# Seven products of a pair in one run: moving the next pair's early products, and the layout of the seeded PSUM banks

## The chip, the cores and the metric

The kernel runs on one core of a Trainium2 chip. The metric is device time in microseconds of one execution. The engines are TensorE (PE; its weight loads are listed as PEld), VectorE (DVE), ScalarE (ACT), GpSimd (POOL) and SyncE (SP), which only starts DMAs here. [...]

## The reference

One step of a single-layer encoder: 512 prompt frames and 64 sample frames, model width 1024, hidden width 4096. After two kinds of attention comes the part that matters here, the feed-forward layer:

```python
x = layer_norm(ALPHA * x + jnp.einsum('blm,md->bld', mix, w_o), ln1_g, ln1_b)
hid = jnp.square(jax.nn.relu(jnp.einsum('bld,df->blf', x, w_up)))
x = layer_norm(ALPHA * x + jnp.einsum('blf,fd->bld', hid, w_down), ln2_g, ln2_b)
gate = jax.nn.sigmoid(jnp.einsum('bld,de->ble', x, w_ple_gate) + b_ple_gate)
```

All of it is f32. The kernel splits each operand into a high and a low part and makes each f32 product from three TensorE passes (high x high, high x low, low x high).

## The kernel before, in words

The 576 frames are two halves A and B of 288 columns. Most of the feed-forward layer is done with Winograd's form of Strassen's product: a block product of 2 x 2 blocks takes seven products instead of eight. A **pair** is one such block product for 256 output rows (two blocks of 128) and both halves. `up_pair` makes hidden rows from x, `down_pair` adds hidden rows times `w_down` into Y. The hidden width is cut into eight groups g of 512. The list `todo` has 24 pairs: four down pairs (hidden groups 0 and 1), then three times four up pairs (g = 2, 3; then 4, 5; then 6, 7; two pairs per group), the first two times followed by four down pairs. Groups 6 and 7 are multiplied by `w_down` in the ordinary way behind the phase (tiles hidE and hidO).

The seven products of a pair have names. Each is 12 matmuls of 128 x 288 into one PSUM bank (four blocks of k, three passes). P.o takes "11", and "t1" and "t2" are added to it (bank n in the profile, two buffers). P.z takes "t0". P.d starts as a copy of P.o after "11" (ACT, line 1466), and "21" is added to it. P.e starts as minus P.o after "t1" (ACT, line 1468); "t3" is added, then DVE reads it, then "22" is added and it is read again. z, d and e all lie in tiles that the profile calls g. Such a g tile has two banks; there are three of them, one from `psB` and two from the ring `psM`.

What reads the banks hangs on `P.posts` and is queued with `later` or `owe`: a queue of work that the loop takes up at its next steps. For an up pair ACT and DVE make relu, square, the sums for the next block product and their high and low parts (tiles hA to hD, hF, r; lines 1325 to 1355); for a down pair DVE adds into Y (lines 1549 to 1564).

Weights come as raw tiles by DMA (`wraw`). A **seven-product** weight has four units u to u+3: "11" and "21" use unit u, "t0" and "t3" u+1, "t1" and "t2" u+2, "22" u+3. For each unit ACT casts the high part (line 149) and DVE subtracts for the low part (line 155), into one of five `whl` slots; DVE also adds raw halves for u+2 (lines 181 and 184). `WT.step()` issues such pieces while products run. A unit may take a slot once the oldest unit still needed is fewer than five behind; `last_use` moves that on after "21", "t3", "t2" and "22".

The products stay in the order in which `seven` issues them (`pin`). Each engine does its own queue in order. Before the change the next pair's "11" and "t0" were taken ahead, between the products of this pair; the first down pair after up pairs (`turn`) has an order and a place for d of its own.

## Time and profile before

| | us |
|---|---|
| median of 3 runs | 784.63 (784.26 to 785.0) |
| the profiled execution | 783.34 |
| its span, first to last instruction | 781.6 |
| PE busy in the span | 755.0 (97%) |
| DVE, ACT busy | 581.2 (74%), 465.5 (60%) |
| seven-product phase, from and to | 382.23 to 672.79 |
| mean granted TensorE clock | 0.990 |

Rows of a timeline give start, duration, engine, line, operation, out<-in, and in brackets the idle time of that engine just before and what ended it. Rows of waits give the total, the number of times and the longest. Rows of windows give the length, each engine's busy time with its instructions in brackets, the granted clock, the DMA share and GB/s.

### The profile page before, as it was taken

What the parts mean: (1) busy time and instruction counts of PE and PEld (TensorE: products, weight loads), DVE (VectorE), ACT (ScalarE), POOL (GpSimd) and SP (SyncE); (2) the same over time, 40 slices, a digit from 0 to 9 for tenths busy, and PEclk for the clock granted to TensorE, in tenths of its full rate; (3) what the DMA queues carried; (4) which work ended last, traced back from release to release, by engine and by line L of the source; (5) the groups of instructions that cost most, each with busy time, mean ns of one, the idle gap of its engine ahead of it and who ended that gap; (6) DMA issues with size and microseconds to landing.
All of it is one profiled execution on the core that took longest, in us unless ns stands there. A gap on an engine that the chain in (4) does not pass through costs nothing.

```text
span 781.6 us, 14647 instructions
## 1 busy us (share of the span) xinstructions
PE 755.0 (97%) x5679; PEld 734.4 (94%) x5679; DVE 581.2 (74%) x1149; ACT 465.5 (60%) x921; POOL 110.1 (14%) x130
## 2 busy tenths in 40 slices
PE   9999999999999999999999996999969999999997
PEld 7999988998999999999899996999969999999997
DVE  6788888888668667988776689665895767658653
ACT  6579767887777433787634566336664366625451
POOL 7100324334321000100000000000000000010100
PEclk9999999999999999999999998999989999999999
DMA  8548354354213235355347664476654764741002
GB/s 279 176 61 171 98 144 129 101 173 129 94 58 117 62 91 167 117 139 130 73 123 185 163 161 123 122 184 160 161 131 122 169 165 139 263 151 32 28 28 68
DMA packets 38200, 101.37 MB, mean 130 GB/s; under 512 B 6001, under 2 KB 10225, under 8 KB 38001
## 3 DMA queue, kind: packets, MB, share of 16 engines
q1 hardware_dynamic: 34384, 87.61, 37.6%
q0 software_dynamic: 3456, 12.58, 9.1%
q8 instruction: 45, 0.74, 0.4%
q10 hardware_dynamic: 288, 0.22, 0.1%
q14 instruction: 27, 0.21, 0.1%
HBM read 85.26 MB, written 9.54 MB: 121 GB/s over the span
## 4 chain that ended last, share of the span: by engine, by line
PE 76%; DVE 15%; ACT 7%; issue 2%; DMA 1%; ACTq 0%; DVEq 0%
PE g L288 40%; PE n L288 14%; PE m L288 13%; DVE dbias L693 2%; PE T L56 2%; ACT xr L771 2%; DVE whl L155 1%; DVE m L691 1%; ACT whl L149 1%; PE V L958 1%; PE m L452 1%; DVE sP L891 1%; PE m L466 1%; DVE x L774 1%; PE S L883 1%
## 5 line engine op out<-in xcount | busy, mean ns | idle before, releaser
L149 ACT CAST whl<-wraw 128x1024 fp32r<-128x1024 f32 (+2 forms) x190 | 154.7, 827 | 112.5 <-PE g L288 81.4
L155 DVE TENSOR_TENSOR whl<-wraw,whl 128x1024 fp32r<-128x1024 f32 (+2 forms) x158 | 158.2, 1008 | 49.5 <-ACT whl L149 49.4
L288 PE MATMUL m<-AH,whl 128*128 128x288 f32 x736 | 176.6, 307 | 0.0
L288 PE MATMUL g<-BH,whl 128*128 128x288 f32 (+2 forms) x768 | 157.6, 296 | 0.0
L288 PEld LDWEIGHTS m<-AH,whl 128*128 128x128 f32 x736 | 126.4, 188 | 1.7 <-issue 1.0
L288 PEld LDWEIGHTS g<-BH,whl 128*128 128x128 f32 x768 | 124.4, 188 | 0.4 <-DVE whl L155 0.2
L288 PE MATMUL g<-BL,whl 128*128 128x288 f32 (+2 forms) x384 | 113.0, 295 | 0.0
L288 PE MATMUL m<-AL,whl 128*128 128x288 f32 x368 | 108.7, 295 | 0.0
L288 PEld LDWEIGHTS g<-BL,whl 128*128 128x128 f32 x384 | 72.3, 188 | 0.2
L288 PEld LDWEIGHTS m<-AL,whl 128*128 128x128 f32 x368 | 69.5, 189 | 0.7
L210 POOL DMA_DIRECT2D wraw<-in_w_dram x24 | 20.8, 866 | 302.9 <-DMA wraw<-in_w_dram 171.0
L896 ACT ACTIVATE sP<-sP,st 128x128 f32<-128x128 f32 (+4 forms) x72 | 39.4, 549 | 35.5 <-DVE st L891 35.4
L155 POOL TENSOR_TENSOR whl<-wraw,whl 128x512 fp32r<-128x512 f32 x32 | 42.3, 1335 | 90.1 <-ACT whl L149 85.3
L288 PE MATMUL m<-BH,whl 128*128 128x288 f32 x192 | 43.0, 302 | 0.0
L288 PE MATMUL g<-s,whl 128*128 128x288 f32 x288 | 42.2, 295 | 0.0
L288 PE MATMUL n<-BH,whl 128*128 128x288 f32 x192 | 42.1, 295 | 0.0
L288 PEld LDWEIGHTS g<-s,whl 128*128 128x128 f32 x288 | 39.5, 188 | 0.2 <-ACT g L1468 0.2
L288 PE MATMUL n<-hA,whl 128*128 128x288 f32 x144 | 24.8, 322 | 11.9 <-DVE whl L155 8.3
L288 PEld LDWEIGHTS n<-hA,whl 128*128 128x128 f32 x144 | 21.9, 207 | 13.8 <-DVE whl L155 9.3
L56 PE MATMUL T<-ident,sP 128*128 128x128 f32 (+1 forms) x176 | 31.3, 273 | 1.5 <-DVE sP L905 0.6
L288 PEld LDWEIGHTS m<-BH,whl 128*128 128x128 f32 x192 | 32.0, 188 | 0.5 <-issue 0.3
L288 PEld LDWEIGHTS n<-BH,whl 128*128 128x128 f32 x192 | 32.0, 188 | 0.0
(322 smaller groups left out, 1623.3 us busy)
## 6 DMA issues: line engine op xcount, KB each, us to landing
wraw<-in_w_dram SPq DMA_DIRECT2D x48, 512.0 KB, 3.7
wraw<-in_w_dram POOLq DMA_DIRECT2D x24, 512.0 KB, 7.2
wraw<-in_w_qkv_dram SPq DMA_DIRECT2D x23, 512.0 KB, 3.7
wraw<-in_w_dram SPq DMA_DIRECT2D x24, 256.0 KB, 6.5
wraw<-in_w_up_dram SPq DMA_DIRECT2D x8, 512.0 KB, 3.5
wraw<-in_w_down_dram SPq DMA_DIRECT2D x8, 512.0 KB, 3.4
wraw<-in_w_gate_dram SPq DMA_DIRECT2D x8, 512.0 KB, 4.8
wraw<-in_w_o_dram SPq DMA_DIRECT2D x8, 384.0 KB, 3.0
```

The costliest lines, as they stand in the source:

```text
L56: PE.transpose(out, in_, ident[:n, :n])
L149: ACT.copy(self.hv[u][:, 0, c], src["tile"][:, c])
L155: eng.tensor_tensor(t[:, 1, c], src["tile"][:, c], f(t[:, 0, c]), OP.subtract)
L210: POOL.dma_start(t[:, :n], it["acc"], accum_op=OP.add)
L288: mm = PE.matmul(ps, W(w, kw, wc), a[:, ka, cols], start=(first and i == 0), stop=(last and i == n - 1), skip_group_check=more)
L452: PE.matmul(mk[:, h, :HW], w0(part, k), a[:, k, h * HW:(h + 1) * HW], start=(k == 0 and i == 0), stop=(k == 7 and i == 2))
L466: PE.matmul(acc[b][:n[b], :304], a[:, k, b * 128:b * 128 + n[b]], ixw(part, k), start=(k == 0 and i == 0), stop=(k == 7 and i == 2))
L691: tc.keep_in_program_order(DVE.max(m, s))
L693: tc.keep_in_program_order(DVE.match_replace(out=s, in_to_replace=m, in_values=s, imm_value=GONE))
L771: q(lambda r=r, s=s: ACT.mul(v2(xr[r * 32:r * 32 + 32]), v[s * 32:s * 32 + 32], sc))
L774: q(lambda: DVE.tensor_tensor(x32, x32, xr, OP.add), 3)
L896: ACT.activation(j["P"], j["P"], AF.Exp, bias=j["st"][:, 0:1], scale=-1.0, accum_out=j["st"][:, 2:3])
```

## The change

Each pair's seven products now follow each other: "11", "t0", "t1", "21", "t3", "t2", "22". Nothing of the next pair comes between. The special order and place of `turn` are gone. z has a `psB` tile of its own use; e of a pair and d of the next pair are the two banks of one `psM` tile: `seeds[0]` is made at "t1", its bank 0 is this pair's e, and its bank 1 is the d that the next pair's "11" seeds. The reads of d and e, which were one instruction over both banks in most pairs, are two: d after "21", e after "22".

```diff
             if n == "11":
                 P.o = psum_n()[:, :HW]
-            if n == ("11" if P.turn else "t0"):
-                P.g = psB.tile([128, 2, 512], F32, name="g", tag="g", bufs=1)
-                P.z = P.g[:, 0, :HW]
+            elif n == "t0":
+                P.z = psB.tile([128, 2, 512], F32, name="g", tag="g", bufs=1)[:, 0, :HW]
...
             if n == "11":
-                P.m = psM.tile([128, 2, 512], F32, name="g", tag="m", bufs=2)
-                P.d, P.e = P.g[:, 1, :HW] if P.turn else P.m[:, 0, :HW], P.m[:, 1, :HW]
+                P.d = seeds[0][:, 1, :HW]
                 ACT.copy(P.d, P.o)
             elif n == "t1":
+                seeds[0] = psM.tile([128, 2, 512], F32, name="g", tag="m", bufs=2)
+                P.e = seeds[0][:, 0, :HW]
                 ACT.mul(P.e, P.o, -1.0)
...
-        yield from product(pairs[0], "11")
-        yield from product(pairs[0], "t0")
-        for i, P in enumerate(pairs):
+        seeds = [psM.tile([128, 2, 512], F32, name="g", tag="m", bufs=2)]
+        for P in pairs:
             if P.start:
                 P.start()
-            for n in ("11+", "t1", "21", "t3", "t2", "t0+", "22") if P.turn else ("21", "t1", "11+", "t3", "t2", "t0+", "22"):
-                if n[-1] != "+":
-                    yield from product(P, n)
-                elif i + 1 < len(pairs):
-                    yield from product(pairs[i + 1], n[:2])
+            for n in ("11", "t0", "t1", "21", "t3", "t2", "22"):
+                yield from product(P, n)
...
+        def s21():
+            later(0, lambda: ACT.activation(P.r[:, 0, 0], P.d, AF.Relu))
+
         def s22():
-            later(0, lambda: ACT.activation(P.r[:, 0], v2(P.m), AF.Relu))
+            later(0, lambda: ACT.activation(P.r[:, 0, 1], P.e, AF.Relu))
...
         def s21():
-            if P.turn:
-                later(0, lambda: begin(ya[:, 0], P.d, OP.add))
+            later(0, lambda: begin(y00, P.d, OP.add))
 
         def s22():
-            if P.turn:
-                later(0, lambda: begin(ya[:, 1], P.e, OP.add))
-            else:
-                later(0, lambda: begin(ya, v2(P.m), OP.add))
+            later(0, lambda: begin(y10, P.e, OP.add))
```

Three places in the built order. The first is TensorE's queue at the start of the phase, as a piece of the difference. A row is a product: n is bank o, g is z, d or e; hA to hD hold the hidden operands ("11" and "t0" read hA, "t1" and "t3" hC, "21" and "t2" hB, "22" hD).

```order
 L288 MATMUL n<-hA,whl 128x288 x12
 L288 MATMUL g<-hA,whl 128x288 x12
-L288 MATMUL n<-hA,whl 128x288 x12
 L288 MATMUL n<-hC,whl 128x288 x12
 L288 MATMUL g<-hB,whl 128x288 x12
 L288 MATMUL g<-hC,whl 128x288 x12
 L288 MATMUL n<-hB,whl 128x288 x12
+L288 MATMUL g<-hD,whl 128x288 x12
+L288 MATMUL n<-hA,whl 128x288 x12
 L288 MATMUL g<-hA,whl 128x288 x12
```

The second pair's "11" moved from the third place to behind the first pair's "22"; between the first pair's "11" and its "t1" only "t0" is left, and between "t3" and "22" only "t2".

The second place is ACT's queue at the first seam from up pairs to down pairs, from the last weight casts of the fourth up pair into the first down pair. Before:

```order
L149 CAST whl_5965<-wraw_5865 128x512
L149 CAST whl_5954<-wraw_5738 128x1024
L1327 CAST hB_5716<-r_5827 128x576
L1327 CAST hC_5814<-hF_5475 128x576
L149 CAST whl_5981<-wraw_5870 128x1024
L1327 CAST hC_5814<-hF_5475 128x576
L1536 ACTIVATE r_5827<-g_5776 128x576
L1537 ACTIVATE r_5827<-r_5827 128x576
L1327 CAST hB_5716<-r_5827 128x576
L1327 CAST hD_5815<-r_5827 128x576
L1466 COPY g_6009<-n_5979 128x288
```

Now:

```order
L149 CAST whl_5967<-wraw_5868 128x512
L1532 ACTIVATE r_5861<-g_5884 128x288
L149 CAST whl_6005<-wraw_5873 128x1024
L1533 ACTIVATE r_5861<-r_5861 128x576
L1327 CAST hB_5687<-r_5861 128x576
L1327 CAST hC_5804<-hF_5444 128x576 x2
L1327 CAST hB_5687<-r_5861 128x576
L1464 COPY g_5884<-n_5949 128x288
L1468 ACTIVATE g_6015<-n_5949 128x288
L1327 CAST hD_5805<-r_5861 128x576
```

whl_5981 before and whl_6005 now are the weights of the second down pair's "11". The copy now belongs to the first down pair itself, whose "t1" is two products behind its "11"; before, the copy in this place was the second down pair's.

The third place is DVE's queue in the first up pair behind the down pairs: the first r<-g row is the read of e after "t3", for which "22" waits. Before:

```order
L155 TENSOR_TENSOR whl_5520<-wraw_5375,whl_5520 128x1024
L184 TENSOR_TENSOR wraw_5378<-wraw_5378 128x512
L1524 TENSOR_TENSOR r_5457<-g_5412,r_5457 128x288
L155 TENSOR_TENSOR whl_5574<-wraw_5378,whl_5574 128x1024
L1527 TENSOR_TENSOR r_5457<-n_5395,r_5457 128x288
```

Now:

```order
L184 TENSOR_TENSOR wraw_5372<-wraw_5372 128x512
L155 TENSOR_TENSOR whl_5537<-wraw_5369,whl_5537 128x1024
L1517 TENSOR_TENSOR r_5479<-g_5502,r_5479 128x288
L155 TENSOR_TENSOR whl_5570<-wraw_5372,whl_5570 128x1024
L1520 TENSOR_TENSOR r_5479<-n_5445,r_5479 128x288
```

The read of e now stands directly behind a 1024-wide weight split, with the sums of raw halves ahead of both.

## The prediction

> **What bounds the kernel now.** I read the page's engine table first, then TensorE's waits from 340 to 700 us, then TensorE's timeline through the seven-product phase, and last ScalarE's (ACT) and VectorE's (DVE) timelines around the places where TensorE stands still. All of them are views of the kernel before.

> ```profile
> PE 755.0 (97%) x5679; PEld 734.4 (94%) x5679; DVE 581.2 (74%) x1149; ACT 465.5 (60%) x921; POOL 110.1 (14%) x130
> ...
> PE n L288 <- DVE whl L155: 8.3, 4, 3.4
> PE n L288 <- ACT whl L149: 3.6, 4, 1.1
> PE g L288 <- DVE Y L1553: 2.1, 1, 2.1
> PE g L288 <- ACT g L1466: 1.0, 1, 1.0
> ```

> TensorE bounds the program, so a change to the order of products can gain only what TensorE loses there. The ten waits sum to 15.0 us; 11.9 of it is product "11" (into a tile n) waiting for a weight split. The timeline shows what the waits cost in all:

> ```profile
> 382.23 1.75 PE L288 MATMUL n<-hA,whl 128*128 128x288 f32 x12
> 384.95 1.86 PE L288 MATMUL g<-hA,whl 128*128 128x288 f32 x12 [0.97 <-ACT g L1466]
> 392.08 1.87 PE L288 MATMUL g<-hB,whl 128*128 128x288 f32 x12 [2.08 <-DVE Y L1553]
> 393.79 1.76 PE L288 MATMUL g<-hC,whl 128*128 128x288 f32 x12
> 400.18 1.76 PE L288 MATMUL g<-hB,whl 128*128 128x288 f32 x12
> 422.52 1.76 PE L288 MATMUL g<-hB,whl 128*128 128x288 f32 x12
> 476.98 1.75 PE L288 MATMUL g<-hA,whl 128*128 128x288 f32 x12
> 481.47 0.53 PE L288 MATMUL n<-hA,whl 128*128 128x288 f32 x2 [1.14 <-ACT whl L149]
> 485.43 2.77 PE L288 MATMUL n<-hA,whl 128*128 128x288 f32 x10 [3.43 <-DVE whl L155]
> 490.28 1.76 PE L288 MATMUL g<-hB,whl 128*128 128x288 f32 x12
> 566.77 1.75 PE L288 MATMUL n<-s,whl 128*128 128x288 f32 x12
> 569.17 0.53 PE L288 MATMUL n<-hA,whl 128*128 128x288 f32 x2 [0.66 <-ACT whl L149]
> 571.86 1.75 PE L288 MATMUL g<-s,whl 128*128 128x288 f32 x12
> 575.05 1.75 PE L288 MATMUL g<-hA,whl 128*128 128x288 f32 x12
> 588.76 1.76 PE L288 MATMUL g<-hB,whl 128*128 128x288 f32 x12
> 666.84 1.10 PE L288 MATMUL g<-hidE,whl 128*128 128x256 f32 x8
> 672.79 7.70 PE L288 MATMUL g<-hidE,whl 128*128 128x256 f32 x64
> ```

> From 400.18 to 422.52 lie 14 products: 22.34 / 14 = 1.596 us each, called T. The phase runs from 382.23 to 672.79, 290.6 us, of which about 1.1 belongs to eight early matmuls of the next stage. Its 24 pairs have 168 products, 168 x 1.596 = 268.1. So the phase **loses 21.4 us**. By place: the start (382.23 to 393.79, 5 products) 11.56 - 7.98 = 3.6; 476.98 to 490.28 (4 products) 13.30 - 6.38 = 6.9; 575.05 to 588.76 (4) 13.71 - 6.38 = 7.3; 566.77 to 571.86 (2) 5.09 - 3.19 = 1.9. The rest, 1.7, is the other place like 569 (the waits table counts four pairs of waits, and the timeline has it at 470). The four places after the start are the two seams from up pairs to down pairs. I call the up pairs of a group U1 to U4 and the down pairs behind them D1 to D4; U3 and U4 are those of odd g.

> At the two long waits more is lost than the wait, because the clock falls:

> ```profile
> 482.00:484.00 2.00, 0.00 (x0) 0.00 (x0) 2.00 (x3) 1.90 (x3) 0.00 (x0) 0.68 0.99 188
> 486.00:488.00 2.00, 2.00 (x11) 2.00 (x10) 1.92 (x4) 0.65 (x1) 0.00 (x0) 0.50 0.02 6
> ```

> (The seventh figure is the granted clock.) After 1.14 and 3.43 us of idle it is 0.50; 6.9 lost against 4.57 waited. After the 2.08 us at 392.08 it did not fall: the product there took 1.71 from start to start (392.08 to 393.79), 0.12 over T. A short wait thus costs itself plus 0.12.

> **What the change removes.** Before, the slot for the weight unit of the next pair's "11" came free with "22" of the pair before, and that "11" came two products later, in a pair with turn (D1) at once: ACT's and DVE's split of it had 3.2 us, or none. At the seam both engines are also splitting hidden operands:

> ```profile
> 480.37 1.05 ACT L149 CAST whl<-wraw 128x1024 fp32r<-128x1024 f32 x1
> ...
> 484.16 1.22 DVE L155 TENSOR_TENSOR whl<-wraw,whl 128x1024 fp32r<-128x1024 f32 x1
> ```

> DVE's split ended at 485.38, 5.2 us after the slot came free, and TensorE went on at 485.43. Now this "11" comes seven products after its slot: 11.2 us against 5.2 there, and against 3.2 plus the wait elsewhere. "t0" and "t1" keep their four products, 6.4. All four seam places go, 17.8 us. At the start, "t0" no longer shares a tile with the copied seed (the 0.97 us) and "21" no longer waits for DVE's reads of z (the 2.08): 3.6 us go. Removed: 21.4.

> **What the change adds.** With no product of the next pair between, three chains get shorter cover. I walked each through the new order with these rows (start to start is an engine's pace, the duration its end):

> ```profile
> 384.50 0.40 ACT L1466 COPY g<-n 128x288 f32<-128x288 f32 x1
> 384.83 0.67 ACT L1327 CAST hB<-r 128x576 fp32r<-128x576 f32 x1
> ...
> 385.98 0.68 ACT L1327 CAST hC<-hF 128x576 fp32r<-128x576 f32 x1
> ...
> 393.98 1.05 ACT L149 CAST whl<-wraw 128x1024 fp32r<-128x1024 f32 x1 [3.55 <-PE g L288]
> ...
> 457.65 0.68 ACT L1537 ACTIVATE hF<-r 128x576 f32<-128x576 f32 x1
> 458.23 1.04 ACT L149 CAST whl<-wraw 128x1024 fp32r<-128x1024 f32 x1
> 459.18 0.66 ACT L1327 CAST hA<-hF 128x576 fp32r<-128x576 f32 x1
> ```
> ```profile
> 393.65 0.72 PEld L288 LDWEIGHTS g<-hC,whl 128*128 128x128 f32 x5
> ```
> ```profile
> 387.20 0.75 DVE L1325 TENSOR_TENSOR hC<-hF,hC 128x576 fp32r<-128x576 f32 x1
> ...
> 395.06 1.23 DVE L155 TENSOR_TENSOR whl<-wraw,whl 128x1024 fp32r<-128x1024 f32 x1 [0.63 <-ACT whl L149]
> 396.21 0.45 DVE L1561 TENSOR_TENSOR Y<-Y,g 128x288 f32<-128x288 f32 x1
> ...
> 466.37 0.75 DVE L1529 SCALAR_TENSOR_TENSOR r<-r 128x576 f32<-128x576 f32 x1
> 467.15 0.76 DVE L1348 SCALAR_TENSOR_TENSOR hF<-hF,r 128x576 f32<-128x576 f32 x1
> 467.83 0.75 DVE L1350 TENSOR_TENSOR hF<-hF,r 128x576 f32<-128x576 f32 x1
> ```

> ACT's pace: a 288-wide copy (taken for the relu of that size too) 0.33, a 576-wide cast or square 0.58, a 1024-wide weight cast 0.95. A product's end reaches ACT 0.19 after the next product starts (393.79, 393.98).

> (1) *Copy before "t1".* "t1" adds into the bank that ACT must first have copied as seed, with only "t0" between: the copy must end 2T - 0.1 = 3.1 us after the pair starts. In a down pair one weight cast stands ahead of it, 0.2 + 0.95, and "11" ends at 1.8: it ends at 2.2, nothing lost. In U4 of the first two groups there stand, after U3's "22": relu 0.33, weight cast 0.95, square 0.58, three operand casts 1.73; 0.2 + 3.59 + 0.40 for the copy = 4.2, and TensorE is about 1.1 + 0.1 late: **1.2, twice**. In D1 there are four operand casts, so the copy ends at 4.8: **1.7, twice**. (Their data come through DVE's row of three 576-wide steps, 0.78 + 0.68 + 0.75; these start when DVE has cleared U4's last split, some 0.7 into the pair, and end at 2.9, before ACT reaches the cast that reads the third, at 3.2.) In U2 and U3 of the last group two hidden-operand casts stand ahead instead: 0.4, twice. Sum 6.6.

> (2) *Add before "22".* "22" adds into the bank from which DVE must first take "t3"; before, "t2" and "t0" lay between, now only "t2". With S the end of "21": ACT's cast S + 0.19, DVE's split S + 1.27, DVE's add S + 2.42 to S + 2.87 (the rows 393.98, 395.06, 396.21 against 393.79, the same chain). TensorE would load the weights for "22" at about S + 3.05 (2T, less the 0.14 that the load at 393.65 stands ahead of its product), and takes 0.05 to notice (485.38, 485.43): a down pair holds with 0.13 in hand. In an up pair the relu of d now comes ahead of the weight cast (before, it was one 576-wide relu after "22"): all 0.33 later, S + 3.20: late by 0.2. Ten of the twelve up pairs (in U4 of two groups the add stands ahead of the split): 2.0. Bounds: 0, if the add lands 0.2 earlier, and 5, if the down pairs miss as well.

> (3) *The first pair.* "t1" needs hC, whose last low part DVE ends at 387.95; unhindered, its seventh matmul would come at 382.23 + 2T + 0.9 = 386.3: 1.7 + 0.1. The second pair's "t1" finds its weights about 0.3 late.

> Added work hidden elsewhere: a second small relu per up pair and a second small add per down pair where one 576-wide did both, 0.1 to 0.2 us each on ACT and DVE, 60% and 74% busy; where they stand in a chain above they are counted. The DMA bytes are the same; a raw tile still has two pairs (22 us) from its release to its cast.

> **Sum.** -21.4 + 6.6 + 2.0 + 2.1 = **-10.7 us**. The profiled execution took 783.34 (span 781.6, 1.7 around it) and would take 772.6; the median of the runs, 784.63, lies 1.3 above it: **774.0**.

> On the clock the profile has two points: 2.08 us idle left it at 1.00, 3.43 us dropped it. [...]

> **The rivals.** A, *slower*: the add before "22" decides in every pair. The place is DVE's queue between "t3" and "22"; it decides once the add ends 0.13 later than in the row. With a second 1024-wide split ahead of it (1.15 more) it costs about 1.1 in each of some 22 pairs, 24 us, of which 2 are in the sum: 774 + 22 = 796; it breaks even at 0.6 a pair. For it: 0.13 is thin. Against: the built order has one split ahead. B, *no change*: the four waits of 1.2 and 1.7 each drop the clock, which cost 2.3 and 2.7 beyond the wait at the long ones: 4 x 2.5 = 10, 784. Against: 392.08. C, *more*: the waits in U4 and D1 do not appear since ACT catches up during "11" and "t0": 774.0 - 5.8 = 768. Against: by the rows every item ahead of the copy is due by then, and ACT does them in order. D, *the shared tile binds what it should not*: the seed copy in one bank waits for DVE's last read of the other bank of that tile. In a down pair that read ends about 0.7 after the pair's start; behind two splits it would end past 3, losing some 0.5 in 12 pairs: 780.

> **How the numbers follow.** Forecast 0.70, own range 770 to 777 (term 2 from 0 to 5, the waits of term 1 half a microsecond shorter each); A 0.08, B 0.07, C 0.09, D 0.06. The range 768 to 781 takes in C and D, and leaves out A and B. A measurement of this kernel tells about 0.2%, 1.6 us, from no change. Faster: forecast, C, D and the part of B where only some waits drop the clock, 0.86; same 0.06; slower 0.08.

> **What would show it.** TensorE's waits for whl into n before the first down pairs gone; no granted clock under 0.9 from 400 to 660 us; in their place four waits of 1.1 to 1.7 us for ACT's copy (line 1464) at the seams, one near 387 us for hC's low part, and some ten of 0.1 to 0.3 us for DVE's line 1517; the phase, 168 products, about 280 us long. Waits for line 1557 in the down pairs would show A, a clock of 0.5 behind a wait under 2 us B, and copies ending late behind line 1547 or 1549 D. The prediction is wrong if a chain that I walked with before's paces runs at another pace.

## The result and the profile after

| | before | after |
|---|---|---|
| median, us | 784.82 (784.26 to 785.44, 4 runs) | 770.76 (770.18 to 771.09, 4 runs) |
| profiled execution, its span | 783.34, 781.6 | 770.57, 768.9 |
| mean granted TensorE clock | 0.990 | 1.000 |
| seven-product phase | 382.23 to 672.79, 1.1 us of it not its own: 289.5 | 381.86 to 659.39: 277.5 |

The ratio is 0.982, 95% interval 0.9803 to 0.9837: the change saves 14.1 us. The prediction was 774.0 us, 768 to 781, faster with a chance of 0.86. Between the two profiled executions the difference is 12.8 us, 12.0 of it in the phase. One of the six executions of the kernel e10 below took 1472 us; it is left out of that kernel's ratio, and its cause is not known.

TensorE's waits from 340 to 700 us, of the changed kernel:

```profile
PE n L288 <- ACT g L1464: 4.6, 4, 1.4
PE n L288 <- DVE hC L1325: 0.9, 1, 0.9
PE n L288 <- ACT hC L1327: 0.3, 1, 0.3
```

15.0 us of waits have become 5.8. The waits for a weight split (lines 149 and 155) into n are gone, and so is the fall of the clock behind them. The four waits for line 1464 are for the copy before "t1", and the clock does not fall behind any of them: it is 1.00 through the whole phase. TensorE's timeline of the changed kernel shows them, and what they cost:

```profile
381.86 1.75 PE L288 MATMUL n<-hA,whl 128*128 128x288 f32 x12
385.04 0.96 PE L288 MATMUL n<-hC,whl 128*128 128x288 f32 x6
386.34 0.40 PE L288 MATMUL n<-hC,whl 128*128 128x288 f32 x1 [0.34 <-ACT hC L1327]
387.64 0.93 PE L288 MATMUL n<-hC,whl 128*128 128x288 f32 x5 [0.90 <-DVE hC L1325]
388.40 1.76 PE L288 MATMUL g<-hB,whl 128*128 128x288 f32 x12
397.97 2.12 PE L288 MATMUL n<-hC,whl 128*128 128x288 f32 x12
399.93 1.76 PE L288 MATMUL g<-hB,whl 128*128 128x288 f32 x12
436.61 0.30 PE L288 MATMUL n<-BH,whl 128*128 128x288 f32 x1
438.25 0.40 PE L288 MATMUL g<-BH,whl 128*128 128x288 f32 x1
439.96 0.29 PE L288 MATMUL n<-BH,whl 128*128 128x288 f32 x1
464.10 1.75 PE L288 MATMUL g<-s,whl 128*128 128x288 f32 x12
466.71 1.85 PE L288 MATMUL n<-s,whl 128*128 128x288 f32 x12 [0.86 <-ACT g L1464]
476.36 1.75 PE L288 MATMUL g<-hA,whl 128*128 128x288 f32 x12
479.52 1.86 PE L288 MATMUL n<-hC,whl 128*128 128x288 f32 x12 [1.42 <-ACT g L1464]
626.48 1.76 PE L288 MATMUL g<-s,whl 128*128 128x288 f32 x12
628.29 1.85 PE L288 MATMUL n<-s,whl 128*128 128x288 f32 x12
659.39 8.64 PE L288 MATMUL g<-hidE,whl 128*128 128x256 f32 x72
```

With 1.596 us for a product, the first "t1" (385.04 to 388.40) loses 1.76, the second pair's (397.97 to 399.93) 0.36, U4's (464.10 to 466.71 for "t0") 1.01, D1's (476.36 to 479.52) 1.56, and the last group's (626.48 to 628.29, in U2 and in U3) 0.21. A "t1" that comes late for the copy also lasts longer itself, 1.85 in place of 1.75, so each of these six costs 0.1 more. The three rows from 436.61 are "t2", "22" and the next pair's "11" of an up pair: 1.64 and 1.71 apart instead of 1.60. That lateness of 0.15 never shows in the table of waits, but it is there in ten of the twelve up pairs.

What stands ahead of the late copy in U4, in ScalarE's timeline of the changed kernel:

```profile
462.72 0.41 ACT L1532 ACTIVATE r<-g 128x288 f32<-128x288 f32 x1 [1.13 <-PE g L288]
463.03 1.05 ACT L149 CAST whl<-wraw 128x1024 fp32r<-128x1024 f32 x1
463.97 0.69 ACT L1533 ACTIVATE r<-r 128x576 f32<-128x576 f32 x1
464.55 0.67 ACT L1327 CAST hC<-hF 128x576 fp32r<-128x576 f32 x1
465.12 0.67 ACT L1327 CAST hB<-r 128x576 fp32r<-128x576 f32 x1
465.69 0.67 ACT L1327 CAST hC<-hF 128x576 fp32r<-128x576 f32 x1
466.26 0.40 ACT L1464 COPY g<-n 128x288 f32<-128x288 f32 x1
```

ScalarE does not pause between the relu and the copy. "11" had ended, and the copy could have started, at about 464.3 (0.19 behind the start of "t0"); it started 2.0 later.

### The profile page after: what moved, and what is told of

It is laid out like the page before. It is cut to its first block, busy times and chain, and to the rows that moved or that the text cites. A ratio compares the mean times of both kernels' runs of the same rounds, so it can differ in the third digit from the quotient of the medians.

```text
span 768.9 us, 14641 instructions
## 1 busy us (share of the span) xinstructions
PE 751.5 (98%) x5679; PEld 730.5 (95%) x5679; DVE 581.1 (76%) x1158; ACT 465.6 (61%) x933; POOL 110.5 (14%) x130
## 4 chain that ended last, share of the span: by engine, by line
PE 75%; DVE 13%; ACT 8%; issue 2%; DMA 1%; ACTq 0%; DVEq 0%
PE g L288 40%; PE m L288 14%; PE n L288 13%; DVE dbias L693 2%; PE T L56 2%; ACT xr L771 2%; ACT whl L149 2%; DVE m L691 1%; PE V L958 1%; DVE whl L155 1%; PE m L452 1%; DVE sP L891 1%; PE m L466 1%; DVE x L774 1%; PE S L883 1%
## 5 line engine op out<-in xcount | busy, mean ns | idle before, releaser
L149 ACT CAST whl<-wraw 128x1024 fp32r<-128x1024 f32 (+2 forms) x190 | 154.8, 828 | 83.3 <-PE g L288 46.8
L155 DVE TENSOR_TENSOR whl<-wraw,whl 128x1024 fp32r<-128x1024 f32 (+2 forms) x158 | 157.7, 1008 | 49.1 <-ACT whl L149 48.5
L288 PE MATMUL m<-AH,whl 128*128 128x288 f32 x736 | 176.7, 307 | 0.0
L288 PE MATMUL g<-BH,whl 128*128 128x288 f32 (+2 forms) x768 | 160.1, 298 | 0.0
L288 PEld LDWEIGHTS m<-AH,whl 128*128 128x128 f32 x736 | 126.4, 188 | 1.7 <-issue 1.0
L288 PEld LDWEIGHTS g<-BH,whl 128*128 128x128 f32 x768 | 125.0, 188 | 1.5 <-DVE whl L155 0.2
L288 PE MATMUL g<-BL,whl 128*128 128x288 f32 (+2 forms) x384 | 113.0, 295 | 0.0
L288 PE MATMUL m<-AL,whl 128*128 128x288 f32 x368 | 108.7, 295 | 0.0
L288 PEld LDWEIGHTS g<-BL,whl 128*128 128x128 f32 x384 | 72.3, 188 | 0.2
L288 PEld LDWEIGHTS m<-AL,whl 128*128 128x128 f32 x368 | 69.5, 189 | 0.6
L155 POOL TENSOR_TENSOR whl<-wraw,whl 128x512 fp32r<-128x512 f32 x32 | 42.2, 1332 | 90.2 <-ACT whl L149 85.3
L288 PE MATMUL m<-BH,whl 128*128 128x288 f32 x192 | 42.9, 302 | 0.0
L288 PE MATMUL g<-s,whl 128*128 128x288 f32 x288 | 42.1, 295 | 0.0
L288 PE MATMUL n<-BH,whl 128*128 128x288 f32 x192 | 42.0, 294 | 0.0
L288 PEld LDWEIGHTS g<-s,whl 128*128 128x128 f32 x288 | 39.4, 188 | 0.0
L288 PEld LDWEIGHTS m<-BH,whl 128*128 128x128 f32 x192 | 32.0, 188 | 0.5 <-issue 0.3
L1468 ACT ACTIVATE g<-n 128x288 f32<-128x288 f32 x24 | 9.5, 395 | 37.3 <-PE n L288 37.3
L288 PEld LDWEIGHTS n<-BH,whl 128*128 128x128 f32 x192 | 32.0, 188 | 0.0
L288 PE MATMUL m<-BL,whl 128*128 128x288 f32 x96 | 28.3, 294 | 0.0
```

What stands on the lines that cost most here:

```text
L149: ACT.copy(self.hv[u][:, 0, c], src["tile"][:, c])
L155: eng.tensor_tensor(t[:, 1, c], src["tile"][:, c], f(t[:, 0, c]), OP.subtract)
L288: mm = PE.matmul(ps, W(w, kw, wc), a[:, ka, cols], start=(first and i == 0), stop=(last and i == n - 1), skip_group_check=more)
L1468: ACT.mul(P.e, P.o, -1.0)
```

## The experiments

Times are medians, with the ratio to the kernel before and its 95% interval. The intervals of e4, e5 and e8 overlap, so what sets these three apart is read from the rows of the one profiled execution of each. The first two take the change apart along its two halves.

**Order back, banks kept** (e1).

```diff
-            for n in ("11", "t0", "t1", "21", "t3", "t2", "22"):
-                yield from product(P, n)
+            for n in ("11+", "t1", "21", "t3", "t2", "t0+", "22") if P.turn else ("21", "t1", "11+", "t3", "t2", "t0+", "22"):
+                if n[-1] != "+":
+                    yield from product(P, n)
+                elif i + 1 < len(pairs):
+                    yield from product(pairs[i + 1], n[:2])
```

> The order of products of the kernel before, its special order for the first down pair included, with the banks and the split reads of the changed kernel. Theory (the order gives back the seams, the banks give back the start): the four seam places lose their 17.8 us again, with two waits near 3.4 us for VectorE's weight split (line 155) into a tile n and the granted clock near 0.5 behind them; the start keeps its gain, less than 1 us lost in place of 3.6; 784.8 - 3.6 = 781 us. Rival (the split reads and the shared tile made the gain): the seams stay free, 774 us or less.

Measured: 812.25 us, 1.0353 (1.0334 to 1.0372). The two long waits at the seams are back (2.8 us each, and a clock of 0.50 from 493.24 and from 602.47 us, for 3.41 us each), as the theory said; the two places with short ones are not. But the time is 31 us above the theory's 781, and above the kernel before. TensorE's waits from 380 to 700 us, its timeline, and ScalarE's:

```profile
PE g L288 <- ACT g L1464: 10.6, 20, 0.6
PE g L288 <- ACT r L1542: 8.3, 9, 1.8
PE g L288 <- DVE Y L1557: 4.4, 8, 0.5
```
```profile
413.83 1.75 PE L288 MATMUL n<-hA,whl 128*128 128x288 f32 x12
416.11 1.86 PE L288 MATMUL g<-hC,whl 128*128 128x288 f32 x12 [0.53 <-ACT g L1464]
```
```profile
415.67 0.38 ACT L1464 COPY g<-n 128x288 f32<-128x288 f32 x1 [1.25 <-PE n L288]
```

The product that waits at 416.11 is "t3", which adds into e. What it waits for is the copy of the next pair's d, in the other bank of the same tile. The two share no data: here order is kept by tile, not by bank, at 10.6 us in 20 such waits. In the same way "21" (into d) waits for the reads of e behind "22" (lines 1542 and 1557, 8.3 and 4.4 us, and line 1559 in the first four down pairs, 2.2). With this order, then, the new banks tie together just what runs side by side.

**Order kept, banks back** (e2).

```diff
-                P.d = seeds[0][:, 1, :HW]
+                P.m = psM.tile([128, 2, 512], F32, name="g", tag="m", bufs=2)
+                P.d, P.e = P.m[:, 0, :HW], P.m[:, 1, :HW]
...
-            later(0, lambda: ACT.activation(P.r[:, 0, 0], P.d, AF.Relu))
-            later(0, lambda: ACT.activation(P.r[:, 0, 1], P.e, AF.Relu))
+            later(0, lambda: ACT.activation(P.r[:, 0], P.m[:, :, :HW], AF.Relu))
```

> The order of the changed kernel, with the banks and the reads of the kernel before: d and e of one pair in one tile, read together behind 22 (for down pairs one 576-wide add, for up pairs one 576-wide relu). Theory (in up pairs the relu of d stands ahead of the weight cast, so that the add before 22 is about 0.15 us late, ten times): 22 of the up pairs starts 1.58 to 1.60 us behind t2 in place of 1.64, and takes 1.59 in place of 1.71; 1.5 us less than the changed kernel's 770.8, 769.3 us. Rival (the tile held until both reads are done delays the next copy): new waits for the copy before t1, 772 us or more. Rival (no difference): 770.8 us, with the 0.15 still there because the weight cast and split alone set it.

Measured: 790.21 us, 1.0068 (1.0053 to 1.0083), slower than the kernel before. TensorE's waits from 340 to 720 us, its timeline and ScalarE's:

```profile
PE g L288 <- ACT g L1467: 13.4, 23, 0.7
```
```profile
410.49 1.76 PE L288 MATMUL n<-hC,whl 128*128 128x288 f32 x12
412.79 1.85 PE L288 MATMUL g<-hB,whl 128*128 128x288 f32 x12 [0.54 <-ACT g L1467]
```
```profile
412.34 0.40 ACT L1467 ACTIVATE g<-n 128x288 f32<-128x288 f32 x1 [2.86 <-PE n L288]
```

In 23 of 24 pairs "21" (into d) waits for line 1467, the seeding of e, which now lies in the same tile and starts only when "t1" ends. Each costs 0.7 to 0.9 us from start to start, 17.6 in all, of the 19.4 that this kernel takes more than the changed one. The rival's cause shows only a little: the copy before "t1" is waited for 1.4 us longer in all than in the changed kernel (line 1465, 6.0 us against 4.6), behind a relu that is now 576 wide. No wait for a weight split is among the waits, and TensorE's timeline of the phase shows no sign of a fall of the clock (a product there lasts 1.86 us at most; in the windows of e6 at a clock of 0.50 it lasts up to 3.25): it is the order that takes the waits for weights away. The small theory of this run did hold: "22" follows "t2" by 1.60 and lasts 1.60 (in U2 "t2", "22" and the next "11" start at 452.08, 453.68 and 455.28). But the large point is one that neither expectation had. Together e1 and e2 give:

| | old banks | new banks |
|---|---|---|
| old order | 784.8 | 812.3 |
| new order | 790.2 | 770.8 |

(784.8 is the kernel before in the first measurement; beside e1 and e2 it took 785.5.) Each half of the change alone makes the kernel slower; together they save 14 us.

**Four slots for split weights instead of five** (e3).

```diff
-    WT.ring(fb, 1, 2, "b", 1)
+    WT.ring(fb, 1, 1, "b", 1)
```

> The changed kernel with four slots for split weights instead of five: in the phase a pair's 11 then gets its slot behind 21 of the pair before, three products (4.8 us) ahead in place of six and more. Theory (at the seams it matters that the split no longer falls into the hidden-operand work behind 22, and a split alone takes 0.2 + 0.95 + 1.2 = 2.4 us): 4.8 us is enough, at most 2 us of waits for whl in the phase, 771 to 773 us, as far as the stages ahead of the phase are not held up by the missing slot. Rival (the lead itself decides: the long seam waits of the kernel before came with a split that was done 5.2 us after its slot): waits for whl of 0.4 us and more before 11 in each first and second down pair, with what the clock adds, 774 us or more in the phase's account.

Measured: 807.83 us, 1.0291 (1.0268 to 1.0313). The phase starts 2.4 us later (384.22) and then takes 33 us more. Its waits from 340 to 720 us, and two of them in TensorE's timeline:

```profile
PE n L288 <- DVE whl L155: 13.8, 11, 1.7
PE n L288 <- ACT whl L149: 12.4, 11, 2.0
```
```profile
445.92 0.54 PE L288 MATMUL n<-s,whl 128*128 128x288 f32 x2 [0.59 <-ACT whl L149]
447.69 2.77 PE L288 MATMUL n<-s,whl 128*128 128x288 f32 x10 [1.24 <-DVE whl L155]
461.02 0.53 PE L288 MATMUL n<-s,whl 128*128 128x288 f32 x2 [0.59 <-ACT whl L149]
462.80 1.60 PE L288 MATMUL n<-s,whl 128*128 128x288 f32 x10 [1.24 <-DVE whl L155]
```

The theory fell, and the rival named the right kind of wait in the wrong place. It is "t1" that waits (n from s or hC), in nine up pairs and the two D1. Its unit u+2 gets its slot only when "t2" of the pair before has ended, and its split is last of three in the queues of ScalarE and VectorE. "11" never waits: for it a lead of 4.8 us is enough, though at the seam of the kernel before the split was done only 5.2 us after its slot. So the length of the lead alone does not decide; it matters too what else ScalarE and VectorE have in their queues then. The clock also falls to 0.50 five times in this kernel, at these waits, for 3.41 us each. One slot less undoes the whole gain and more.

**ScalarE's copy ahead of the hidden-operand casts** (e4).

```diff
-            if e[0] > clock[0]:
+            if e[0] > clock[0] or hold[0] and e[3]:
                 break
...
-                P.o = psum_n()[:, :HW]
+                P.o, hold[0] = psum_n()[:, :HW], True
...
-                ACT.copy(P.d, P.o)
+                hold[0] = ACT.copy(P.d, P.o) is None
```

> The changed kernel, with the hidden-operand casts held back while an 11 runs, so that ScalarE's copy of its bank stands ahead of them in the fourth up pair and the first down pair. Theory (the copy is late before t1 only because of the casts queued ahead of it): the waits for line 1464, 4.6 us in all, go; in the first down pairs t1 then waits up to 0.3 us for hC; 770.8 - 4.5 = 766.3 us. Rival (the place of the casts only moves the wait, since t1, 21 or the weight splits then wait for the operands): waits for hB, hC or whl of 0.8 us and more at the same places, 769 to 772 us.

Measured: 768.72 us, 0.9793 (0.9774 to 0.9811); the phase (382.38 to 657.81) takes 275.4 us against 277.5. ScalarE's timeline at D1 (the copy, now ahead of all four casts), and TensorE's waits from 340 to 720 us:

```profile
476.22 0.40 ACT L1464 COPY g<-n 128x288 f32<-128x288 f32 x1
```
```profile
PE n L288 <- DVE hC L1325: 1.9, 3, 0.9
PE n L288 <- DVE whl L155: 1.3, 2, 0.6
```

The theory holds as to the cause: no wait for the copy is left at the seams (0.2 us stays before "t1" in U2 and U3 of the last group, whose casts are not held back here). The rival holds as to half of the gain: D1's "t1" now waits 0.5 us for hC, and D2's "t1" 0.6 for its weights. 2.1 us came of the 4.5.

**The relu of d on VectorE** (e5), on top of e4:

```diff
-            later(0, lambda: ACT.activation(P.r[:, 0, 0], P.d, AF.Relu))
+            later(0, lambda: DVE.tensor_scalar(P.r[:, 0, 0], P.d, 0.0, None, op0=OP.max))
```

> The kernel of the copy-first experiment (768.7 us), with the relu of d in up pairs done by VectorE instead of ScalarE, so that ScalarE's cast of the weights behind 21 starts 0.3 us earlier. Theory (that relu ahead of the cast is what makes 22 of up pairs late): 22 starts 1.58 to 1.60 us behind t2 in place of 1.64 and takes 1.59 in place of 1.71; ten times 0.15 us, 767.2 us. Rival (the add before 22 is late for another reason, such as the split ahead of it on VectorE): 22 stays 0.15 late, 768.7 us. Rival (VectorE, now with 0.4 us more in each up pair, becomes late itself): new waits for whl or for VectorE's add, above 769 us.

Measured: 767.75 us, 0.9791 (0.9778 to 0.9805); the phase takes 274.7 us, 0.7 less than e4's. The lateness of "22" is gone, as TensorE's timeline shows at the end of "t2" and the start of "22" in U1:

```profile
438.41 0.29 PE L288 MATMUL n<-BH,whl 128*128 128x288 f32 x1
438.54 0.29 PE L288 MATMUL g<-BH,whl 128*128 128x288 f32 x1
```

They lie one matmul's pace apart, 0.13 (in the changed kernel the same two lie 0.17 apart, and the next matmul follows after 0.24). So the relu ahead of the weight cast is what made "22" late in these ten pairs. In U4 of the first two groups the second rival came true instead: "22" waits 0.4 us for VectorE's line 1517, twice. Whether the added relu makes this wait is open here; e10 below has the wait without it.

**Many short waits** (e6) and **a few long ones** (e7): the copy of the seed is done several times over, to the same effect, so that "t1" is late.

```diff
-                ACT.copy(P.d, P.o)
+                for _ in range(1 + 6 * (pairs.index(P) not in (0, 7, 8, 15, 16))):
+                    ACT.copy(P.d, P.o)
```

In e7 the count is 9, 10, 12, 13, 14 and 16 more in pairs 2, 5, 10, 13, 18 and 21, and none elsewhere.

> The changed kernel, with ScalarE's copy of the seed done seven times over in 19 pairs (all but the first, and those beside the two seams), so that TensorE waits some 1.1 us before t1 in each (the copy lands 2.16 us into a pair, six more take 2.0, and t1 is due at 3.05). Theory (the clock falls only where TensorE stands still for more than about 1.6 us within one of the fixed stretches of 3.41 us that the falls of the other runs lie on): no fall; the waits cost themselves and 0.12 each, 19 x 1.22 = 23 us, 794 us. Rival B of the prediction (many short waits swing the clock): the granted clock falls to 0.5 behind most of them, for 3.41 us each, 19 x 1.7 = 32 us more, about 826 us.

Measured: 827.39 us, 1.0548 (1.0534 to 1.0563). The figure meets rival B's, but not for its reason. Copies into one bank follow each other at 0.41 us, not 0.33 (seven took 2.87), and in up pairs other work of ScalarE came between. TensorE's waits from 380 to 720 us are these:

```profile
PE n L288 <- ACT g L1465: 45.9, 23, 3.6
```

So 41 us more was waited than in the changed kernel, against 21 planned. In the timeline fourteen of the waits last 1.38 to 1.70 us, one in every pair of about 12.8 us, and no fall of the clock follows any of them, nor the one of 2.90; six last 3.43 to 3.61, and the clock fell to 0.50 at each. Rival B of the prediction is out for waits as short as the change has, 1.42 us at most.

> The changed kernel, with the copy of the seed repeated in six pairs so often that TensorE waits about 2.1, 2.4, 3.1, 3.4, 3.7 and 4.4 us before t1 there. Theory (fixed stretches of 3.41 us, and a fall behind each in which TensorE was busy for about half or less): the waits of 3.4 us and more drop the clock wherever they lie, those of 2.1 and 2.4 us only where 1.6 us of them lie in one stretch; all falls and rises lie a whole number of 3.41 us apart. Rival (the length of a single wait decides, between 2.08 and 3.43 us as in the kernel before): the falls begin with the end of a wait of a certain length, at no fixed distance from each other, and the waits of 2.1 and 2.4 us drop nothing.

Measured: 810.65 us in a single execution. The waits became 2.62, 5.09, 3.87, 6.34, 4.70 and 7.76 us; the clock fell to 0.50 at all but the first. What the falls have in common is told under the last heading.

**The second pair's "11" third at the start** (e8), on top of e4, with the last group's casts held back too:

```diff
-            for n in ("11", "t0", "t1", "21", "t3", "t2", "22"):
-                yield from product(P, n)
+            for n in ("11", "t0", "11+", "t1", "21", "t3", "t2", "22") if P is pairs[0] else ("11", "t0", "t1", "21", "t3", "t2", "22")[P is pairs[1]:]:
+                yield from product(pairs[1] if n[-1] == "+" else P, n[:2])
```

> The kernel of the copy-first experiment (768.7 us), with the second pair's 11 taken third at the start of the phase, as in the kernel before, and with the casts of the last group's hidden operands held back behind the copy too. Theory (the first t1 waits 1.7 us for the low part of hC, and another product in front of it covers that; the wait of 0.2 us before t1 in the third and fourth pair of the last group is the copy behind casts): 768.7 - 1.7 - 0.4 = 766.6 us. Rival (21 of the first pair, which reads hB, is then late, or the second pair's weights): a new wait of 0.5 us and more within the first 15 us of the phase, 768 us or more.

Measured: 767.59 us, 0.979 (0.9777 to 0.9804); the phase takes 274.7 us, 0.7 less than e4's. The wait of 0.2 us in the last group is gone (twice), and the first "t1" loses 0.2 in place of 1.7. But the second pair's "t1" now loses 1.9 in place of 0.4. From VectorE's timeline of this kernel:

```profile
394.92 3.07 DVE L155 TENSOR_TENSOR whl<-wraw,whl 128x512 fp32r<-128x512 f32 x3
```

VectorE has worked since 383.2 without a pause, and three splits stand in a row here; the second pair's "t1" needs the last of them. The rival was right as to the wait (its time, 768 us or more, was missed by 0.4): VectorE is the bound at the start of this kernel.

**Together** (e9 to e11, on one chip): the changed kernel again, then e4 with the relu of d on VectorE except in U4 (the condition `g % 2 and m` below takes in the last group's U4 too) and the last group's casts held back, then that with e8's start.

```diff
-            later(0, lambda: ACT.activation(P.r[:, 0, 0], P.d, AF.Relu))
+            later(0, lambda: ACT.activation(P.r[:, 0, 0], P.d, AF.Relu) if g % 2 and m else DVE.tensor_scalar(P.r[:, 0, 0], P.d, 0.0, None, op0=OP.max))
```

> The changed kernel again, beside the next two, so that they are compared on one chip: 770.8 us by its first runs, 0.982 of the kernel before.

> The copy-first kernel with the relu of d on VectorE in every up pair but the fourth of the first two groups (where VectorE's queue made 22 wait 0.4 us twice), and the last group's casts held back as well. Theory (each of these waits has the one cause named): against the copy-first kernel 1.5 us less before 22 and 0.4 us less before t1, no wait for line 1517 left; 768.7 - 1.9 = 766.8 us, 4 us less than the changed kernel. Rival (VectorE's work only moves to the next wait, at hC or at a weight split of the first and second down pairs): 1 us less at most, 767.8 us and more.

> The kernel of the run above with the second pair's 11 taken third at the start of the phase. Theory (at the start VectorE bounds: it is busy from 383 to 400 us, so a wait covered at the first t1 comes back at the second pair's t1, as 0.5 + 0.9 us for whl): no difference to the run above beyond 0.5 us. Rival (covering the first t1 does gain its 1.7 us): 1.5 us less than the run above.

| | us | ratio to before | phase, us |
|---|---|---|---|
| e9, the changed kernel | 770.18 | 0.9819 (0.9806 to 0.9832) | 277.5 |
| e10 | 766.85 | 0.9774 (0.9762 to 0.9787) | 273.5 |
| e11, with the other start | 766.65 | 0.9772 (0.9759 to 0.9784) | 273.4 |

e10 comes out where its theory put it, but by another way: "22" of U4 still waits for line 1517 (1.3 us in two waits), while the waits for hC in D1 and for the weights in D2, left out of the sum, fell from 0.8 and 0.9 us lost to 0.3 and 0.4. That the sum came out is luck. VectorE's timeline shows what U4 waits for, in e10 and then in e4:

```profile
470.60 1.22 DVE L155 TENSOR_TENSOR whl<-wraw,whl 128x1024 fp32r<-128x1024 f32 x1
471.73 0.75 DVE L1325 TENSOR_TENSOR hD<-r,hD 128x576 fp32r<-128x576 f32 x1
472.40 0.45 DVE L1517 TENSOR_TENSOR r<-g,r 128x288 f32<-128x288 f32 x1
```
```profile
471.19 0.46 DVE L1517 TENSOR_TENSOR r<-g,r 128x288 f32<-128x288 f32 x1
```

In e4 the read of e stands ahead of the low part of hD (471.56) and of a 1024-wide split (472.24), and "22" does not wait. In e5 and e10 it stands behind both. In e10 ScalarE does this pair's relu again, and the wait is longer than in e5, 0.6 against 0.4. So the order of VectorE's queue is enough to make the wait, without the relu that e10's theory blamed; why the order changed is not shown.

e11 shows again that the start gains nothing: what its first "t1" saves, the second pair's loses. Both are faster than the changed kernel; the intervals of e10 and e9 do not meet.

## Why the prediction was right

The forecast, 774.0, lies 3.2 us above the measured 770.76, on the right side and inside its range. Step by step:

- **Removed, 21.4 us.** Right: every wait and every fall of the clock that the sum counted is gone, at the start and at both seams.
- **The copy before "t1", 6.6 us.** Right in place and cause (e4 shows the cause), a little high in each size: with the 0.1 by which the late "t1" itself lasts longer, 1.1 in U4 against 1.2, 1.66 in D1 against 1.7, 0.3 against 0.4 in the last group, 6.2 in all. The sum took the copy as due when TensorE loads weights, 3.1 us into the pair; by the rows the loss runs from where "t1" itself would start, 3.19. The 0.1 for the restart is in the sum for U4 but was left out for D1, where the two slips nearly cancel. For the 0.4 of the last group the prediction shows no working.
- **The add before "22", 2.0 us.** 1.6: late by 0.16 in ten of the twelve up pairs (prediction 0.2), in down pairs not at all, as the 0.13 in hand said. Its cause, the relu ahead of the cast, is shown by e5 and by e2.
- **The first pairs, 2.1 us.** 1.76 and 0.36.

These rows add up to 9.9 us. By the length of the phase (277.5 us against 168 products of 1.596) 9.4 us were added where 10.7 were forecast, since a product that nothing delays takes 1.592 rather than 1.596; the phase gained 12.0. Of the 3.2 us between forecast and result 1.3 are this difference. The rest is outside the sum: the phase starts 0.4 us earlier, the stages behind it took 0.4 less, and the median lies 0.2 above the profiled execution where the forecast added the 1.3 of the kernel before.

Of the rivals, A (the add decides in every pair) did not come: no wait for line 1557. B is out by its own sign, since the clock is 1.00 through the phase, and e6 says the same of waits of that length. C (no copy waits) is out by the table of waits; even with the copy ahead, half of that gain came back as other waits. D never showed: no copy is late behind a read of line 1547 or 1549.

One reading of the prediction was too narrow, though the sum did not rest on it. It treated the new bank layout as something that could only bind (rival D), or free the start. e1 and e2 show that it carries the change: in consecutive order "21" follows "t1" directly, and in the old tiles it waits for the seed of e in 23 pairs, 13.4 us in all (e2). The prediction's own walk through the old order could have told this. There, "21" stood ahead of "t1", and "11" of the next pair lay between "t1" and "t3".

## What to carry to other kernels

Where a program orders work by tile, as this one does (e1 and e2), the banks that share a tile must be used one behind the other, and which those are follows from the order of the products. Change the order and the tiling together, and test each half alone before crediting either. A wait that is removed by a reorder can come back as the next chain's short cover (here 15.0 us of waits went, and 5.8 came in other places): walk each chain through the new queues, item by item, with the old rows' paces; here that gave the places, and sizes within 0.2 us. A lead that is counted in products (a slot, a buffer) is only worth what the queues of the helping engines leave of it: in e3 4.8 us were enough for "11", and "t1" waited up to 2.0 us for its weights.

## What was not expected of the hardware

```profile
444.13:447.54 3.41, 1.73 (x11) 1.26 (x10) 2.59 (x4) 2.71 (x5) 0.87 (x1) 1.00 0.51 186
447.54:450.95 3.41, 3.26 (x13) 3.26 (x14) 0.77 (x2) 0.40 (x1) 0.00 (x0) 0.50 0.82 133
461.19:464.61 3.42, 2.18 (x15) 1.94 (x16) 2.22 (x3) 0.93 (x3) 0.84 (x1) 1.00 0.57 103
```

And of e6, and e7 (whose first wait, 2.62 us, dropped nothing); behind both of these the clock stayed at 1.00:

```profile
437.11:440.53 3.42, 1.85 (x14) 1.61 (x14) 0.98 (x2) 1.82 (x6) 0.00 (x0) 1.00 1.01 213
```
```profile
408.00:411.41 3.41, 1.63 (x13) 1.39 (x11) 2.91 (x5) 3.07 (x9) 0.84 (x1) 1.00 0.76 214
```

In the kernel before, e1, e3, e6 and e7, from about 388 to 700 us, every stretch at full clock with 1.84 us busy or more kept it, and every one with 1.55 or less lost it; of the three between them one kept it (1.63, e7) and two lost it (1.64, e1; 1.73, e3), which the busy figure does not separate. (At half clock more was needed: those with up to 2.53 us busy, in e6, stayed there, and those with 3.04, in e7, and more rose.) The changed kernel's longest wait, 1.42 us, left 1.99 busy in the 3.41 us from 477.20, which hold all of it: more than any stretch that lost the clock had. The 2.08 us before, which the prediction took as harmless, were a matter of where they lay: across two stretches, with 2.85 and 1.89 us busy, which both kept the clock. All in one stretch of 3.41 they would have left 1.33, less than the 1.55 that lost it.

**The kernel before scatters more.** Its executions beside the experiments reach from 782.8 to 786.0 us, those of the changed kernel from 770.0 to 771.1. The time goes with the mean clock of each execution. Beside the experiments 18 executions of the kernel before had 0.988 and took 785.1 us in the mean, 12 had 0.990 and took 783.7; by the figures above, one stretch of 3.41 us at a clock of 0.50 is 0.002 of the mean clock and 1.7 us. The changed kernel's executions had 0.999 to 1.000. Where the falls lay is known for the one profiled execution alone, so why the executions differ is not shown.
